# One forward substitution for all eight chunks of a pair of heads, instead of one for each half of four

## The chip, the cores and the metric

The kernel runs on one core of one Trainium2 chip. The metric is the device time of one launch in microseconds (us), the median of several runs. The engines are named as the profile names them: PE is TensorE's matmul, PEld its weight load, DVE is VectorE, ACT is ScalarE, POOL is GpSimd, SP issues the DMAs. A line such as L783 is a line of the profiled kernel.

## The reference, cut to what matters

One decoder layer at 512 tokens and width 2048, all in float32:

```python
h = modulate(rms_norm(x, norm_mix_g), sh_m, sc_m)
p = h @ w_in                                   # columns: RG-LRU, its gate, RWKV-7
y_a = rg_lru(conv(p_lru)) * gelu(p_gate)       # 1024 channels
y_b = rwkv7_mix(p_rwkv)                        # 1024 channels, 16 heads of 64
x = x + g_m * (concat(y_a, y_b) @ w_out)
h = modulate(rms_norm(x, norm_ffn_g), sh_f, sc_f)
x = x + g_f * ((silu(gate) * up) @ w_down)     # gate, up = h @ w_gu
return rms_norm(x, final_norm_g)
```

Inside `rwkv7_mix` a head's 64 x 64 state goes through the tokens one at a time:

```python
sa = state @ (-kk_t)
state = state * d_t + sa (kk_t * a_t)^T + v_t k_t^T
y_t = state @ r_t
```

## The kernel before, in words

Features lie on the 128 partitions, the 512 tokens on the free axis. A float32 product is made of three products of exactly split operands (`mm3`, L124 to L126), each 128x128 by 128x512. I call one of these three a large product. Weights come in by SP (L115), are rounded by ACT (L105), and DVE makes the remainder (L106).

The recurrence is done in chunks of 64 tokens, eight chunks, for two heads at a time (a pair; there are eight pairs). For each chunk and head it needs the inverse of a unit triangular 64 x 64 matrix I - A. This is done by a forward substitution in the two diagonal 32-blocks, on DVE, and by two small products for the block below them.

For each pair these pieces run:

- `rwkv_main`: what all tokens need (decays, normalized keys), once per pair.
- `rwkv_half`: operands and products of four chunks (L609 to L657), twice per pair. Its products are L624 (values by token), L633 and L643 (products within the chunks), L655 (transposes). `rw_dg` holds the diagonal 32-blocks.
- `inverse`: directly behind each `rwkv_half`. DVE spreads the blocks by a transpose (`rw_at`, L757), sets `rw_x` from a constant (L760), and makes 31 steps of a product (L764, `rw_xp`) and a sum (L766, `rw_x`). Two more transposes give `rw_xn` (L768) and `rw_xs` (L771). POOL copies `rw_xs` into `bd_xt` (L775). TensorE makes the lower block by L783 and L793, with ACT copies behind each (L787, L796).
- `rwkv_chain`: the state goes through the eight chunks one after the other. In each chunk, w = a product of the state (L694, L696) copied by ACT (L698), u = `bd_xt` times w (L701) copied by ACT (L703), the new state (L708, L709 on TensorE, L719 on ACT, L720 on DVE), and the output (L710, L712, L713). At the end a group norm and a gate (L729 to L745), and `y` is written to DRAM (L746).

The order is set by `weave`. It holds several generators in a list, traces the next step of the first one that may run by its own clock (constants such as `INVLAT`), and otherwise one step of a filler: three large products of work that does not hang on the chain. The filler has the rest of the input projection, the RG-LRU half, and the products of `y_a` with its half of `w_out` (`project(self.ya, 1, "mm")`). When all of `weave` has been traced, `channel` begins: it reads `y_b` back from DRAM (L439, tiles `yraw`, `yhi`, `ylo`), multiplies it with the other half of `w_out`, and makes the norm (L230, L240) and the feed-forward part. A scheduler may still move instructions within an engine. Each engine then works its own queue in order.

A pair's second half may be built only when the previous pair's chain has left the last chunk, because `bd_a`, `bd_bt` and `bd_v` are held once per half; the first half, when it has left the fourth.

Of the kernel before, what the change touches and what calls it, by code (L numbers as in the profile page):

```python
# [17 lines left out]
P = 128  # L18
S = 512
# [32 lines left out]
for _n, _k in _VEC:  # L52
# [4 lines left out]
# columns of the constants (shapes alone)  # L57
_CON = [("ident", 128), ("center", 128), ("bones", 128),
        ("gmask", 128), ("xinit", 128), ("m01", 2)]
# [8 lines left out]
def _constants():  # L68
    con = np.zeros((P, NCON), np.float32)
    p = np.arange(P)  # L70
    blk = (p[:, None] // C == p[None, :] // C).astype(np.float32)
    con[:, _COFF["ident"]:][:, :P] = np.eye(P, dtype=np.float32)
    con[:, _COFF["center"]:][:, :P] = np.eye(P, dtype=np.float32) - blk / C
    con[:, _COFF["bones"]:][:, :P] = blk
    s, t = (p % C)[:, None], np.arange(C)[None, :]
    con[:, _COFF["gmask"]:][:, :C] = s < t
    con[:, _COFF["gmask"] + C:][:, :C] = s <= t
    r = ((p % 32) // 4)[:, None, None]
    con[:, _COFF["xinit"]:][:, :P] = (
        np.arange(32)[None, :, None] == 8 * np.arange(4)[None, None, :] + r).reshape(P, P)  # L80
    q = (p // 32) % 2
    con[:, _COFF["m01"]] = q == 0
    con[:, _COFF["m01"] + 1] = q == 1
    return con


class Layer:
# [24 lines left out]
    def load_split(self, src, n):  # L112
        """src: DRAM [128, n] -> (hi, lo) float32r tiles [128, n]"""
# [14 lines left out]
    def gemm_steps(self, ps, src, acts):  # L128
        """ps[128, S] = W^T acts, src: DRAM [128, nk * 128], acts: list of (hi, lo); yields after each k"""
# [44 lines left out]
    def mod_pair(self, j):  # L174
        """columns j and j + 16"""
# [11 lines left out]
    def mod_steps(self, js, pool, tags):  # L187
        """the same for many columns, a quarter of c at a time"""
# [22 lines left out]
    def mod_scale(self, col, sc, g):  # L211
        """col = g * (1 + mod[:, sc])"""
# [3 lines left out]
    def square(self, acc, x, k, pool):  # L216
        """acc += x * x"""
# [7 lines left out]
    def norm(self, acc, tag):  # L225
        """1 / rms of each token, in all partitions (PSUM), from sums of squares by partition"""
# [16 lines left out]
    def modulate(self, x, col, rstd, sh, lo=None):  # L243
        """hi, lo of x * col * rstd + sh"""
# [54 lines left out]
    def mixing(self):  # L299
# [22 lines left out]
                # seven tiles stay in PSUM, four more take turns in the last bank by quarters of K  # L322
# [43 lines left out]
    def rwkv_weave(self, kvr0, kvr1, u0):  # L366
# [16 lines left out]
        def filler():  # L383
# [15 lines left out]
            # half of the channels through the output projection  # L399
# [23 lines left out]

        def chains():
            for pr in range(NPAIR):
                yield 0, 0, lambda: done["inv"] > 2 * pr
# [3 lines left out]
        self.weave([chains(), halves(0), halves(1), mains(), mods()], self.filler)  # L430
# [14 lines left out]
    def project(self, ys, half, *tags):  # L445
        """x1 += g_m * (ys through their half of w_out)"""
# [29 lines left out]
    def rwkv_setup(self, ctx):  # L476
# [4 lines left out]
        # zero at the first token of each chunk  # L481
# [3 lines left out]
        # block-diagonal operands (two heads); what lies off the blocks stays zero  # L485
# [36 lines left out]
    def rwkv_main(self, pr):  # L522
        """what a pair of heads needs of all the tokens"""
# [16 lines left out]
        # decay and its running product within a chunk  # L540
# [21 lines left out]
        # kk = k * k_k over its norm per head  # L562
# [15 lines left out]
        # k' = k (1 + (a - 1) k_a), the bonus, v by tokens  # L578
# [17 lines left out]
    def rwkv_half(self, pr, hf):  # L596
        """four chunks of a pair"""
# [21 lines left out]
        # v by tokens, centred over its features  # L619
# [9 lines left out]
        # products within the chunks  # L629
# [6 lines left out]
        d = rw.tile([P, 4, 32], F32, tag=f"dg{hf}", name="rw_dg")  # L636
# [40 lines left out]
        # through the chunks  # L677
# [49 lines left out]
        # group norm (y is centred already), bonus, gate  # L727
# [22 lines left out]
    def inverse(self, hf, dg, gb):  # L750
        """bd["xt"][hf]: the transposed inverse of I - A of each head and chunk, A^T in gb[:, :, :C]"""
# [3 lines left out]
        # diagonal 32-blocks, one to a partition (eight partitions share its columns)  # L755
        at = rw.tile([P, 32, 32], F32, tag=f"at{hf}", name="rw_at")
        nc.vector.transpose(  # L757
            out=at, in_=dg.rearrange("p c t -> p t c").unsqueeze(2).to_broadcast([P, 32, 8, 4]))
        x = rw.tile([P, 32, 4], F32, tag=f"x{hf}", name="rw_x")
        nc.vector.tensor_copy(out=x.rearrange("p t j -> p (t j)"), in_=self.con("xinit"))  # L760
# [6 lines left out]
        xn = rw.tile([P, 32, 4], F32, tag=f"at{hf}", name="rw_xn")      # [t, j, chunk]  # L767
        nc.vector.transpose(out=xn.rearrange("p (j r) c -> p j (r c)", r=8),  # L768
                            in_=x.rearrange("p t j -> p j t"))
        xs = rw.tile([P, 4, 32], F32, tag=f"dg{hf}", name="rw_xs")      # [j, chunk, t]  # L770
        nc.vector.transpose(out=xs, in_=xn.rearrange("p j c -> p c j"))  # L771
        xt = self.bd["xt"][hf]
        for g in range(4):
            rows = slice(g * 32, g * 32 + 32)
            nc.gpsimd.tensor_scalar(out=xt[rows, :, rows], in0=xs[rows], scalar1=1.0,  # L775
                                    scalar2=None, op0=ALU.mult)
        yield 0, INVLAT, None
        # lower left blocks: X21 = X22 A21 X11
        ps = self.ps("gr").rearrange("p (c x) -> p c x", x=P)
        for c in range(4):  # L780
            for g in range(2):
                q0, q1 = slice(g * C, g * C + 32), slice(g * C + 32, g * C + C)
                mm(ps[q1, c, :32], lhsT=gb[q0, c, 32:C], rhs=xn[q0, :, c], start=True, stop=True)  # L783
        rt = rw.tile([P, 4, 32], F32, tag=f"x{hf}", name="rw_rt")
# [3 lines left out]
        yield 0.43, HOP, None  # L788
        ps = self.ps("gr").rearrange("p (c x) -> p c x", x=P)
        for c in range(4):  # L790
# [3 lines left out]
        for g in range(2):  # L794
# [251 lines left out]
```

## Time and profile before

| | us |
|---|---|
| median of 3 runs | 2511.28 (2510.93 to 2513.99) |
| span of the profiled execution | 2515.8 |
| PE busy in the span | 2413.9 (96%) |
| DVE busy in the span | 1380.4 (55%) |
| ACT busy, POOL busy | 843.7 (34%), 82.0 (3%) |

The profiled execution is one run of its own; the page gives its span, from the first to the last instruction, and no other time for it. It stands 4.5 us above the median of the runs. Three stages matter here. Until about 225 us the input is normalized and the first products are made. From 225 to 939 us `weave`'s steps and filler run. From 939 us the products of `y_b` follow (norm at 1041 us), and then the feed-forward part to the end.

### The profile page before, as it was taken

Reading aid. Unit: us, or ns where it says so; the run is one execution under the profiler, and the core shown is the slowest. Engines: PE = TensorE matmul, PEld = TensorE weight load, DVE = VectorE, ACT = ScalarE, POOL = GpSimd, SP = SyncE. Lnnn points to the kernel's source line nnn. Section 1 sums busy time; section 2 is a strip of 40 time slices with the busy share of each in tenths; the row PEclk is TensorE's granted clock in tenths of the full one; section 3 lists DMA queues with packets and bytes.
Section 4 is the critical chain, followed back from the end, with each engine's and each line's share of the span. In section 5 each row is a group of like instructions: output and inputs, shape, how many; then the busy total and the mean of one; then the engine's idle time right before and its main releaser. Section 6 shows DMA issues by size and latency. Waiting matters only on the chain.

```text
span 2515.8 us, 30983 instructions
## 1 busy us (share of the span) xinstructions
PE 2413.9 (96%) x11560; PEld 1953.4 (78%) x11560; DVE 1380.4 (55%) x3111; ACT 843.7 (34%) x1340; POOL 82.0 (3%) x131
## 2 busy tenths in 40 slices
PE   5999999999999999899999999999999999999997
PEld 3677777877777886687788888888888888888885
DVE  7979898999969847854423322233322233222244
ACT  4357364455355333432222222222222222222221
POOL 0000111111101000000000000000000000000000
PEclk9999998999999999999999999999999999999998
DMA  8864444444342438366423332323333233333233
GB/s 304 308 219 130 148 128 143 131 152 144 125 135 81 143 108 283 119 195 194 160 90 95 108 100 93 101 83 98 106 98 99 89 92 105 101 93 100 85 95 112
DMA packets 138938, 333.22 MB, mean 132 GB/s; under 512 B 15458, under 2 KB 28898, under 8 KB 134690
## 3 DMA queue, kind: packets, MB, share of 16 engines
q1 hardware_dynamic: 138788, 331.25, 40.7%
q8 instruction: 90, 1.47, 0.2%
q14 instruction: 60, 0.49, 0.1%
HBM read 322.92 MB, written 7.87 MB: 131 GB/s over the span
## 4 chain that ended last, share of the span: by engine, by line
PE 72%; DVE 9%; DMA 7%; issue 1%; ACT 1%; SPq 0%; POOL 0%; DVEq 0%; ACTq 0%
PE ps_mm L124 10%; PE ps_mm L126 10%; PE ps_mm L125 10%; PE ps_gr L126 6%; PE ps_st L124 6%; PE ps_gr L124 6%; PE ps_st L126 6%; PE ps_gr L125 6%; PE ps_st L125 6%; DMA adaq<-in_w_ada 6%; DVE adaq L199 2%; DVE wlo L106 2%; DVE rw_xp L764 1%; DVE rw_x L766 1%; DMA wraw<-in_w_out 1%
## 5 line engine op out<-in xcount | busy, mean ns | idle before, releaser
L106 DVE TENSOR_TENSOR wlo<-wraw,whi 128x1024 fp32r<-128x1024 f32 (+2 forms) x552 | 496.7, 902 | 730.2 <-ACT whi L105 721.1
L105 ACT CAST whi<-wraw 128x1024 fp32r<-128x1024 f32 (+2 forms) x552 | 436.6, 792 | 1292.4 <-PE ps_mm L125 401.1
L124 PE MATMUL ps_mm<-hhi,whi 128*128 128x512 f32 x1020 | 417.1, 410 | 9.8 <-ACT hhi L251 7.2
L126 PE MATMUL ps_mm<-hhi,wlo 128*128 128x512 f32 x1020 | 407.2, 399 | 1.7 <-DVE wlo L106 1.6
L125 PE MATMUL ps_mm<-hlo,whi 128*128 128x512 f32 x1020 | 406.5, 399 | 0.8 <-DVE hlo L252 0.7
L124 PEld LDWEIGHTS ps_mm<-hhi,whi 128*128 128x128 f32 x1020 | 193.4, 190 | 53.2 <-ACT hhi L251 9.9
L125 PEld LDWEIGHTS ps_mm<-hlo,whi 128*128 128x128 f32 x1020 | 193.7, 190 | 43.4 <-DVE hlo L252 4.8
L126 PEld LDWEIGHTS ps_mm<-hhi,wlo 128*128 128x128 f32 x1020 | 193.8, 190 | 42.3 <-DVE wlo L106 3.0
L199 DVE SCALAR_TENSOR_TENSOR adaq<-adaq,cbq 128x512 f32<-128x512 f32 x256 | 173.5, 687 | 92.9 <-DMA adaq<-in_w_ada 85.1
L126 PE MATMUL ps_gr<-hhi,wlo 128*128 128x512 f32 x496 | 193.7, 390 | 3.1 <-DVE wlo L106 3.1
L126 PE MATMUL ps_st<-hhi,wlo 128*128 128x512 f32 x496 | 193.6, 390 | 2.0 <-DVE wlo L106 2.0
L124 PE MATMUL ps_st<-hhi,whi 128*128 128x512 f32 x496 | 194.0, 391 | 1.6 <-ACT hhi L251 1.6
L125 PE MATMUL ps_gr<-hlo,whi 128*128 128x512 f32 x496 | 193.5, 390 | 0.0
L125 PE MATMUL ps_st<-hlo,whi 128*128 128x512 f32 x496 | 193.5, 390 | 0.0
L124 PE MATMUL ps_gr<-hhi,whi 128*128 128x512 f32 x496 | 192.6, 391 | 0.0
L126 PEld LDWEIGHTS ps_gr<-hhi,wlo 128*128 128x128 f32 x496 | 93.4, 188 | 23.6 <-DVE wlo L106 4.1
L126 PEld LDWEIGHTS ps_st<-hhi,wlo 128*128 128x128 f32 x496 | 93.4, 188 | 21.8 <-DVE wlo L106 2.5
L124 PEld LDWEIGHTS ps_st<-hhi,whi 128*128 128x128 f32 x496 | 93.5, 188 | 21.6 <-ACT hhi L251 2.2
L125 PEld LDWEIGHTS ps_gr<-hlo,whi 128*128 128x128 f32 x496 | 93.7, 189 | 19.6
L124 PEld LDWEIGHTS ps_gr<-hhi,whi 128*128 128x128 f32 x496 | 93.7, 189 | 19.4
L125 PEld LDWEIGHTS ps_st<-hlo,whi 128*128 128x128 f32 x496 | 93.3, 188 | 19.8 <-DVE hlo L252 0.3
L766 DVE TENSOR_TENSOR rw_x<-rw_x,rw_xp 128x27 f32<-128x27 f32 (+23 forms) x496 | 94.7, 196 | 5.7
(312 smaller groups left out, 3809.6 us busy)
## 6 DMA issues: line engine op xcount, KB each, us to landing
wraw<-in_w_gu SPq DMA_DIRECT2D x176, 512.0 KB, 3.6
adaq<-in_w_ada SPq DMA_DIRECT2D x256, 256.0 KB, 3.3
wraw<-in_w_in SPq DMA_DIRECT2D x160, 256.0 KB, 3.0
ada<-in_w_ada SPq DMA_DIRECT2D x32, 1024.0 KB, 7.2
wraw<-in_w_down SPq DMA_DIRECT2D x64, 512.0 KB, 3.5
wraw<-in_w_out SPq DMA_DIRECT2D x64, 256.0 KB, 3.3
wraw<-in_w_down SPq DMA_DIRECT2D x64, 192.0 KB, 2.3
x<-in_x SPq DMA_DIRECT2D x32, 256.0 KB, 5.3
```

Source lines behind the costliest of these rows:

```text
L105: nc.scalar.copy(out=hi, in_=src)
L106: nc.vector.tensor_tensor(out=lo, in0=src, in1=hi.bitcast(F32), op=ALU.subtract)
L124: mm(ps, lhsT=w[0], rhs=x[0], start=start, stop=False)
L125: mm(ps, lhsT=w[0], rhs=x[1], start=False, stop=False)
L126: self.pe = mm(ps, lhsT=w[1], rhs=x[0], start=False, stop=stop).ins
L199: nc.vector.scalar_tensor_tensor(out=t, in0=t, scalar=1.0, in1=cb, op0=ALU.mult, op1=ALU.mult, accum_out=part[:, m, h:h + 1])
L764: tt(out=pr[:, :n, :j], in0=at[:, s + 1:, s:s + 1].to_broadcast([P, n, j]), in1=x[:, s:s + 1, :j].to_broadcast([P, n, j]), op=ALU.mult)
L766: tt(out=x[:, s + 1:, :j], in0=x[:, s + 1:, :j], in1=pr[:, :n, :j], op=ALU.add)
```

## The change

`inverse` is taken out of `rwkv_half` and becomes a generator of its own, one step of which runs when both halves of a pair are built. It substitutes for all eight chunks at once: each partition now holds one of 4 groups of columns instead of 8, and step s works on `s // 4 + 1` columns instead of `s // 8 + 1`. The chain of a pair starts when the whole inverse is done, where before it started when the first half's was done and asked for the second at chunk 4. `INVLAT` goes from 30.2 to 24.0.

```diff
-INVLAT = 30.2                   # substitution in the diagonal blocks
+INVLAT = 24.0
...
+        def inverses():
+            for pr in range(NPAIR):
+                yield 0, 0, lambda: done["built"] == 2 * pr + 2
+                yield from self.inverse(*self.pairs[pr][-1])
+
         def chains():
             for pr in range(NPAIR):
-                yield 0, 0, lambda: done["inv"] > 2 * pr
+                yield 0, 0, lambda: done["inv"] > pr
                 yield from self.rwkv_chain(pr)
...
-        self.weave([chains(), halves(0), halves(1), mains(), mods()], self.filler)
+        self.weave([chains(), inverses(), halves(0), halves(1), mains(), mods()], self.filler)
...
-        d = rw.tile([P, 4, 32], F32, tag=f"dg{hf}", name="rw_dg")
+        if hf == 0:
+            parts.append(rw.tile([P, NCH, 32], F32, tag="dg", name="rw_dg"))
+        d = parts[0][:, 4 * hf:4 * hf + 4]
...
-        yield from self.inverse(hf, d, gb)
...
-            if c == 4:
-                yield 0, 0, lambda: self.done["inv"] >= 2 * pr + 2
-            ar, gb, rkt, bn, kn = parts[hf]
+            ar, gb, rkt, bn, kn = parts[1 + hf]
...
-            out=at, in_=dg.rearrange("p c t -> p t c").unsqueeze(2).to_broadcast([P, 32, 8, 4]))
-        x = rw.tile([P, 32, 4], F32, tag=f"x{hf}", name="rw_x")
-        pr = rw.tile([P, 31, 4], F32, tag=f"dg{hf}", name="rw_xp")
+            out=at, in_=dg.rearrange("p c t -> p t c").unsqueeze(2).to_broadcast([P, 32, 4, NCH]))
+        x = rw.tile([P, 32, 8], F32, tag="x", name="rw_x")
+        pr = rw.tile([P, 31, 8], F32, tag="xp", name="rw_xp")
         for s in range(31):
-            n, j = 31 - s, s // 8 + 1
+            n, j = 31 - s, s // 4 + 1
             tt(out=pr[:, :n, :j], in0=at[:, s + 1:, s:s + 1].to_broadcast([P, n, j]),
                in1=x[:, s:s + 1, :j].to_broadcast([P, n, j]), op=ALU.mult)
             tt(out=x[:, s + 1:, :j], in0=x[:, s + 1:, :j], in1=pr[:, :n, :j], op=ALU.add)
...
-        yield 0.43, HOP, None
+        yield 0.86, HOP, None
```

The two small products (L783 and L793 before, L788 and L798 after) now cover eight chunks in one step, and POOL's copies come eight in a row instead of four. TensorE has the same instructions as before, in another order; no DMA is added or taken away.

What stands in the queues shows where work moved. The line numbers of the changed kernel are some 5 higher. The first place is TensorE's queue at the end of the weave. Before, the last pair's gate (L743, L744), like every step of its chain ahead of it, stands between large products of the filler:

```order
L126 MATMUL ps_mm<-yhi,wlo 128x512
L743 MATMUL ps_ch<-lora_g,rw_lwg 128x512
L744 MATMUL ps_ch<-lora_s,rw_lws 128x512
L124 MATMUL ps_mm<-yhi,whi 128x512
L125 MATMUL ps_mm<-ylo,whi 128x512
```

In the changed kernel the filler's last large product (the first row) stands ahead of the last pair's second half (L629 to L662), its inverse (L788, L798) and its whole chain (from L705 on):

```order
L126 MATMUL ps_mm<-yhi,wlo 128x512
L629 MATMUL ps_st<-cons,mix_v 64x64 x8
L638 MATMUL ps_gr<-rw_ar,bd_b_1390 128x128 x4
L650 MATMUL ps_gr<-rw_ar,bd_k_1392 128x128 x4
L747 MATMUL ps_ch<-lora_g,rw_lwg 128x512
L748 MATMUL ps_ch<-lora_s,rw_lws 128x512
L662 MATMUL ps_st<-cons,bd_b_1390 128x128 x4
L698 MATMUL ps_ch<-bd_v_1402,bd_bt_1398 128x128
L662 MATMUL ps_st<-cons,bd_k_1392 128x128 x4
L714 MATMUL ps_y<-rw_rkt,bd_v_1402 128x64
L788 MATMUL ps_gr<-rw_xn,rw_gb 32x32 x16
L798 MATMUL ps_gr<-rw_xs,rw_rt 32x32 x16
```

From L705 on, eight chunks and the group norm follow without one large product among them; the next one is the first of `y_b`. Before, 39 large products of the filler were left behind the last pair's gate (L744).

The second place is DVE's queue in the substitution. Before, for instance in the sixth pair, steps of the substitution (here the last ones of a half) stand among weight splits (L106) and partial columns of the modulation (L199):

```order
L766 TENSOR_TENSOR rw_x<-rw_x,rw_xp 128x16
L199 SCALAR_TENSOR_TENSOR adaq,adaparts<-adaq,cbq 128x512
L764 TENSOR_TENSOR rw_xp<-rw_at,rw_x 128x12
L766 TENSOR_TENSOR rw_x<-rw_x,rw_xp 128x12
L764 TENSOR_TENSOR rw_xp<-rw_at,rw_x 128x8
```

In the changed kernel's last pair the steps stand alone from the third of the 62 on, up to the two transposes:

```order
L768 TENSOR_TENSOR rw_xp<-rw_at,rw_x 128x16
L770 TENSOR_TENSOR rw_x<-rw_x,rw_xp 128x16
L768 TENSOR_TENSOR rw_xp<-rw_at,rw_x 128x8
L770 TENSOR_TENSOR rw_x<-rw_x,rw_xp 128x8
L772 STREAM_TRANSPOSE rw_xn<-rw_x 128x256
```

In the other seven pairs the substitution still stands among splits and modulation columns, and 123 to 208 large products stand on TensorE between a pair's second half (L650) and its L788.

More of the change, by code (lines that the diff above doesn't have):

```diff
@@ L58 @@
 _CON = [("ident", 128), ("center", 128), ("bones", 128),
-        ("gmask", 128), ("xinit", 128), ("m01", 2)]
+        ("gmask", 128), ("xinit", 256), ("m01", 2)]
 _COFF = {}
@@ L77, in _constants @@
     con[:, _COFF["gmask"] + C:][:, :C] = s <= t
-    r = ((p % 32) // 4)[:, None, None]
-    con[:, _COFF["xinit"]:][:, :P] = (
-        np.arange(32)[None, :, None] == 8 * np.arange(4)[None, None, :] + r).reshape(P, P)
+    r = ((p % 32) // 8)[:, None, None]
+    con[:, _COFF["xinit"]:][:, :256] = (
+        np.arange(32)[None, :, None] == 4 * np.arange(8)[None, None, :] + r).reshape(P, 256)
     q = (p // 32) % 2
@@ L748, in rwkv_chain, with inverse @@
         yield 1.07, 2.0, None
-    def inverse(self, hf, dg, gb):
+    def inverse(self, dg, *parts):
         nc, rw = self.nc, self.rw
@@ L754, in inverse @@
         tt = nc.vector.tensor_tensor
-        at = rw.tile([P, 32, 32], F32, tag=f"at{hf}", name="rw_at")
+        at = rw.tile([P, 32, 32], F32, tag="at", name="rw_at")
         nc.vector.transpose(
-            out=at, in_=dg.rearrange("p c t -> p t c").unsqueeze(2).to_broadcast([P, 32, 8, 4]))
-        x = rw.tile([P, 32, 4], F32, tag=f"x{hf}", name="rw_x")
-        nc.vector.tensor_copy(out=x.rearrange("p t j -> p (t j)"), in_=self.con("xinit"))
-        pr = rw.tile([P, 31, 4], F32, tag=f"dg{hf}", name="rw_xp")
+            out=at, in_=dg.rearrange("p c t -> p t c").unsqueeze(2).to_broadcast([P, 32, 4, NCH]))
+        x = rw.tile([P, 32, 8], F32, tag="x", name="rw_x")
+        nc.vector.tensor_copy(out=x.rearrange("p t j -> p (t j)"), in_=self.con("xinit", 256))
+        pr = rw.tile([P, 31, 8], F32, tag="xp", name="rw_xp")
         for s in range(31):
-            n, j = 31 - s, s // 8 + 1
+            n, j = 31 - s, s // 4 + 1
             tt(out=pr[:, :n, :j], in0=at[:, s + 1:, s:s + 1].to_broadcast([P, n, j]),
@@ L766, in inverse @@
             tt(out=x[:, s + 1:, :j], in0=x[:, s + 1:, :j], in1=pr[:, :n, :j], op=ALU.add)
-        xn = rw.tile([P, 32, 4], F32, tag=f"at{hf}", name="rw_xn")
-        nc.vector.transpose(out=xn.rearrange("p (j r) c -> p j (r c)", r=8),
+        xn = rw.tile([P, 32, NCH], F32, tag="at", name="rw_xn")
+        nc.vector.transpose(out=xn.rearrange("p (j r) c -> p j (r c)", r=4),
                             in_=x.rearrange("p t j -> p j t"))
-        xs = rw.tile([P, 4, 32], F32, tag=f"dg{hf}", name="rw_xs")
+        xs = rw.tile([P, NCH, 32], F32, tag="xp", name="rw_xs")
         nc.vector.transpose(out=xs, in_=xn.rearrange("p j c -> p c j"))
[L772 to L776, printed above, removed]
+        for hf in range(2):
+            for g in range(4):
+                rows = slice(g * 32, g * 32 + 32)
+                nc.gpsimd.tensor_scalar(out=self.bd["xt"][hf][rows, :, rows], in0=xs[rows, 4 * hf:4 * hf + 4],
+                                        scalar1=1.0, scalar2=None, op0=ALU.mult)
         yield 0, INVLAT, None
-        ps = self.ps("gr").rearrange("p (c x) -> p c x", x=P)
-        for c in range(4):
+        ps = self.ps("gr").rearrange("p (c x) -> p c x", x=C)
+        for c in range(NCH):
+            gb = parts[c // 4][1]
             for g in range(2):
                 q0, q1 = slice(g * C, g * C + 32), slice(g * C + 32, g * C + C)
-                mm(ps[q1, c, :32], lhsT=gb[q0, c, 32:C], rhs=xn[q0, :, c], start=True, stop=True)
-        rt = rw.tile([P, 4, 32], F32, tag=f"x{hf}", name="rw_rt")
+                mm(ps[q1, c, :32], lhsT=gb[q0, c % 4, 32:C], rhs=xn[q0, :, c], start=True, stop=True)
+        rt = rw.tile([P, NCH, 32], F32, tag="x", name="rw_rt")
         for g in range(2):
@@ L787, in inverse @@
             nc.scalar.copy(out=rt[q1], in_=ps[q1, :, :32])
-        yield 0.43, HOP, None
-        ps = self.ps("gr").rearrange("p (c x) -> p c x", x=P)
-        for c in range(4):
+        yield 0.86, HOP, None
+        ps = self.ps("gr").rearrange("p (c x) -> p c x", x=C)
+        for c in range(NCH):
             for g in range(2):
@@ L793, in inverse @@
                 mm(ps[q0, c, :32], lhsT=rt[q1, c, :], rhs=xs[q1, c, :], start=True, stop=True)
-        for g in range(2):
-            q0, q1 = slice(g * C, g * C + 32), slice(g * C + 32, g * C + C)
-            nc.scalar.copy(out=xt[q0, :, q1], in_=ps[q0, :, :32])
-        yield 0.43, 1.4, None
+        for hf in range(2):
+            for g in range(2):
+                q0, q1 = slice(g * C, g * C + 32), slice(g * C + 32, g * C + C)
+                nc.scalar.copy(out=self.bd["xt"][hf][q0, :, q1], in_=ps[q0, 4 * hf:4 * hf + 4, :32])
+        yield 0.86, 1.4, None
         self.done["inv"] += 1
```

## The prediction

> **What bounds the kernel now.** I read the page first, then the busy time by stage, then TensorE's waits in the stage that the change touches. The page says that TensorE is the bound of the whole:
>
> ```profile
> span 2515.8 us, 30983 instructions
> PE 2413.9 (96%) x11560; PEld 1953.4 (78%) x11560; DVE 1380.4 (55%) x3111; ACT 843.7 (34%) x1340; POOL 82.0 (3%) x131
> ```
>
> By stage (span, then busy time of each engine, granted clock, DMA share, GB/s) it is less simple:
>
> ```profile
> 225.00:939.00 714.00, 685.63 (x4048) 550.23 (x4043) 602.99 (x1967) 350.68 (x689) 71.32 (x106) 0.97 0.41 128
> 939.00:1041.00 102.00, 92.76 (x387) 70.76 (x387) 78.39 (x182) 35.32 (x56) 0.00 (x0) 1.00 0.76 253
> 1041.00:2516.00 1475.00, 1446.69 (x6368) 1194.86 (x6368) 514.80 (x656) 350.90 (x426) 0.00 (x0) 0.99 0.34 107
> ```
>
> The first row is the weave. TensorE is busy for 686 of 714 us, DVE for 603, and the granted clock is 0.97. DVE's load is the one that the change lowers. So the next view is what TensorE waits for there (total us, times, longest), and what one such wait does, by the timeline and by two stretches around it:
>
> ```profile
> PE ps_gr L783 <- DVE rw_xn L768: 18.7, 8, 3.7
> PE ps_st L568 <- ACT rw_t L566: 2.5, 2, 2.2
> PE ps_gr L783 <- DVE rw_x L766: 0.6, 1, 0.6
> ...
> 433.23 0.66 PE L783 MATMUL ps_gr<-rw_xn,rw_gb 32*32 32x32 f32 x16 [3.71 <-DVE rw_xn L768]
> ...
> 433.00:443.00 10.00, 9.77 (x51) 6.31 (x52) 5.95 (x23) 6.54 (x13) 2.84 (x4) 0.51 0.46 140
> 443.00:453.00 10.00, 10.00 (x64) 8.72 (x63) 9.24 (x36) 5.81 (x13) 0.00 (x0) 1.00 0.39 128
> ```
>
> TensorE waits 19.3 us (18.7 + 0.6) for the substitution's result, in nine of its sixteen halves. Behind the 3.71 us wait the clock is 0.51 for 10 us, so it costs about 5 us more. Over the stage, 0.03 of 714 us is 21 us lost to the clock, and I put it all down to these waits. The price of DVE's lateness is then about 19 + 21 = 40 us. The rest of the 714 us is TensorE's own work, so relief of DVE can take about 40 us and no more.
>
> **The change, part by part.**
>
> *DVE's work.* Where a half's step stands alone, starts follow each other by the dependence and not by the size:
>
> ```profile
> 843.05 0.20 DVE L766 TENSOR_TENSOR rw_x<-rw_x,rw_xp 128x45 f32<-128x45 f32 x1
> 843.29 0.20 DVE L764 TENSOR_TENSOR rw_xp<-rw_at,rw_x 128x42 f32<-128x42 f32 x1
> 843.53 0.20 DVE L766 TENSOR_TENSOR rw_x<-rw_x,rw_xp 128x42 f32<-128x42 f32 x1
> ...
> 850.65 0.17 DVE L764 TENSOR_TENSOR rw_xp<-rw_at,rw_x 128x12 f32<-128x12 f32 x1
> 850.86 0.17 DVE L766 TENSOR_TENSOR rw_x<-rw_x,rw_xp 128x12 f32<-128x12 f32 x1
> ```
>
> That is 0.24 us at 42 elements and 0.21 at 12. The new shapes have 8 to 76 elements, mean 50 (1560 elements in 31 steps, against 920 before). The slope of 0.03 us in 30 elements gives 0.24 to 0.25 at 50. So 62 steps take about 15 us per pair where two halves took twice 14. On DVE the change saves some 13 us per pair of steps alone in the queue, and about 2 us for the second spreading transpose, 8 x 15 = 120 us at most. It saves less where another instruction stands between two steps, since then the wait was filled.
>
> *The waits at L783.* Eight inverses remain where sixteen were, and the last pair's is counted below. With 7/16 of the 40 us they would cost 18. DVE has less behind it, so I take 11 left: a gain of 29 us. The bounds are 40 (none left) and 10 (each of the seven waits is as long as the 3.71 us one, clock included).
>
> *The tail.* In the new order the filler's last large product stands ahead of the last pair's second half. From there until `y_b`'s products nothing covers the chain. I add up that stretch from rows of before, starting at the second half's first product (L624):
>
> ```profile
> 852.06 0.69 PE L624 MATMUL ps_st<-cons,mix_v 128*64 128x64 f32 x16
> 852.67 1.16 PE L633 MATMUL ps_gr<-rw_ar,bd_b 128*128 128x128 f32 x8
> 853.67 1.06 PE L643 MATMUL ps_gr<-rw_ar,bd_k 128*128 128x128 f32 x8
> 856.34 0.60 PE L655 MATMUL ps_st<-cons,bd_b 128*128 128x128 f32 x4
> 857.93 2.05 DVE L757 STREAM_TRANSPOSE rw_at<-rw_dg 128x1024 f32<-128x1024 f32 x1
> 862.82 0.65 PE L783 MATMUL ps_gr<-rw_xn,rw_gb 32*32 32x32 f32 x16
> 864.98 0.44 PE L793 MATMUL ps_gr<-rw_xs,rw_rt 32*32 32x32 f32 x16
> 865.47 0.52 ACT L796 COPY bd_xt<-ps_gr 32x128 f32<-32x128 f32 x2 [0.68 <-PE ps_gr L793]
> ...
> L775 POOL TENSOR_SCALAR bd_xt<-rw_xs 32x128 f32<-32x128 f32 x64 | 39.9, 623 | 287.2 <-DVE rw_xs L771 142.1 <-DVE rw_xp L764 123.9 <-DVE rw_x L766 17.8
> ...
> 570.52 0.38 PE L701 MATMUL ps_ch<-rw_w,bd_xt 128*128 128x128 f32 x2
> 570.74 0.39 PE L708 MATMUL ps_ch<-bd_v,rw_kn 128*128 128x128 f32 x2
> 571.26 0.49 PE L709 MATMUL ps_ch<-rw_u,rw_bn 128*128 128x128 f32 x2
> 572.13 0.35 DVE L720 SCALAR_TENSOR_TENSOR rw_s<-ps_ch,rw_pcs,rw_w 128x128 f32<-128x128 f32 x1
> 572.73 0.38 PE L696 MATMUL ps_ch<-rw_s,bd_a 128*128 128x128 f32 x2
> 572.95 0.33 PE L710 MATMUL ps_y<-rw_rkt,bd_v 128*128 128x64 f32 x2
> 573.12 0.39 PE L712 MATMUL ps_y<-rw_ar,rw_s 128*128 128x64 f32 x2
> 573.64 0.39 PE L701 MATMUL ps_ch<-rw_w,bd_xt 128*128 128x128 f32 x2
> ...
> 923.66 1.02 PE L732 MATMUL ps_ch<-rw_t,cons 128*128 128x512 f32 x2
> 929.32 1.02 PE L743 MATMUL ps_ch<-lora_g,rw_lwg 128*128 128x512 f32 x2
> 931.50 0.33 SPq L746 DMA_DIRECT2D y<-rw_t  x1
> 937.06 1.20 ACT L105 CAST yhi<-yraw 128x512 fp32r<-128x512 f32 x2
> ...
> 939.28 0.39 PE L124 MATMUL ps_mm<-yhi,whi 128*128 128x512 f32 x1
> 1040.88 1.07 PE ps_ch L230 x8
> ```
>
> 1. L624 to the spreading transpose: 857.93 - 852.06 = 5.9 us, with the same group norm of the pair before between them on DVE.
> 2. The transpose 2.0, what is left of that norm 2.2 (four instructions of 0.3 to 0.7), 62 steps 14.9, the transpose to `rw_xn` 0.5: 19.6, so `rw_xn` stands at 25.5 us.
> 3. L783 to L793 2.2, to ACT's copies 0.5, two copies 0.5: 28.7. POOL's first four copies (4 x 0.62, behind `rw_xs` at about 26) end at the same time; the other four are needed only at chunk 4.
> 4. Seven chunks at 3.12 us (573.64 - 570.52, a pair with little between its steps) and a last one of 1.3, with the norm's square: 21.8 + 1.3 + 0.7, so L732 stands at 52.5 us.
> 5. L732 to the write of `y`: 7.8 before, less some 1.9 us of splits and `x1` sums that are no longer between, plus about 1 for a halved clock: 7.0, so the write is issued at 59.5 us.
> 6. From that write to the norm: 1040.88 - 931.50 = 109.4 us as before. SP goes straight from the write to the reads of `y_b` (yhi 5.6 us later), DVE and ACT go from the gate to the splits, and the loads and modulation columns that paced that stage before follow in the same order. I add 2 us for large products that begin at a low clock.
>
> The sum is 171 us from the filler's last product to the norm. Before, from the filler's last product (939.28) to the norm was 101.6 us. The tail adds 69 us. For the chunk I take the 3.12 us: closest in kind, since hardly anything stands between its steps. Its bounds are 2.5 (0.4 us between the end of L709 and L720 and 0.2 us between the end of L720 and L696, in which other work went ahead) and 3.5 (clock at a half, 0.2 us more on two products of the cycle). Seven chunks make that -4 to +3 us, and steps 3 and 5 are open by 3 us each.
>
> *The covered work that goes.* The last pair's second half, inverse and chain were between filler products and took TensorE's time there. From start to start these are 0.6 + 1.0 + 1.0 + 2 x 0.5 for the half and 2 x (0.6 + 0.4) for the inverses. A chunk has five wide fp32 products (0.22, L701 to L708) and three narrow ones (0.17, L710 to L712), 1.6, eight times 12.9; norm and gate take 2 x 1.0. Together that is 21 us that the covered stretch no longer holds. They are inside the 171.
>
> *Costed at nothing.* POOL's eight copies in a row: 5 us, of which chunk 0 needs the first four, and filler products lie behind L788 in the first seven pairs. The first chunks of a pair wait for the whole inverse: the filler covers it until it runs out, and that is the tail. SP: no DMA is added, and what is queued behind a waiting one is a weight load that runs three tiles ahead.
>
> On the clock the row is 0.51 for 10 us behind a 3.71 us wait. The Trainium skill (TensorE: Matmul & The Clock Gate, Part 1) says that the array falls to half speed after an idle window of about 3.4 us and comes back after as long a busy one. By it the whole substitution in the tail (some 17 us without a product) ends at half clock, and the chunks may stay there: 3.5 us each, a sum 3 us above mine; were the clock full, 4 us below. The trace agrees on the fall; no row here shows a chain of small products alone.
>
> **The sum.** +69 (tail) - 21 (moved out of the covered stretch) - 29 (waits and clock) = +19 us. Against the profiled execution that is a span of 2535; the runs' median is 4.5 lower, so 2511.3 + 19 = 2530.
>
> **The rivals.**
>
> *DVE was the true bound, and the tail is cheap* (faster). The place is the tail, its price 69. For it: DVE is busy 84% of the weave, and all nine waits are for it. If all 40 us go and the tail is 10 us shorter: 69 - 10 - 21 - 40 = -2. It decides in favour of faster only if the tail adds less than 61 at full gain, or less than 50 at mine. Against it: each step of the tail is a row, and a chain of 8 chunks is on it. At its end, 20 us off the tail, the time is 2499.
>
> *Gain and tail cancel* (no change): 2506 to 2516, which needs 14 us off my sum, for instance all waits gone and a tail of 65.
>
> *The waits stay* (slower still). For it: one late inverse now holds up eight chunks, and L788's place in the queue is set by estimates, as L783's was. Seven waits with their clock, 7 x 5 = 35 us, leave a gain of 5, and the sum is +43: 2554.
>
> *The change does not reach the queue*: the order shows that it does. I give it nothing.
>
> **How the numbers follow.** The forecast, slower by 8 to 32 us (2519 to 2543), has 0.62; the waits staying, over 2543, 0.16; cancelling, 0.12; faster by over 5 us (0.2%, about what a measurement of this kernel tells from no change) 0.08. The rest, slower by 5 to 8, has 0.02. Faster is then 0.08, same 0.12, slower 0.80. The range leaves out one in ten on each side: 2508 to 2553. The predicted time is the forecast's 2530.
>
> **What the changed profile would show.** If I am right, the slices of TensorE's busy time have one hollow stretch of about 60 us, from about 890 to 950 us, with some 17 us nearly empty first and small products alone after that, at a lowered clock; TensorE's longest waits are L788 on `rw_xn` once for some 17 us, and L705, L713 and L700 on ACT and DVE in the last pair. The filler's last large product ends at about 890 instead of 939 us (939 - 21 - 29), the norm L230 stands at about 1060. DVE's busy time falls by 70 to 120 us, and the other seven waits for `rw_xn` sum to under 8 us. I would be wrong if large products stood in the tail, if the filler's end came before 870 (DVE held up more than its waits show), or if the seven waits were as long as before.

## The result and the profile after

The changed kernel takes 2557.82 us (median of 4 runs, 2553.32 to 2559.96), the kernel before 2511.86 beside it: a ratio of 1.018, 95% interval 1.0165 to 1.0194. That is 46 us slower, where 19 were forecast. The direction and the place were right; the size was not, and the time lies 5 us above the forecast's range.

The page's head and three of its rows in 40 slices (64 us each; 9 is 90% or more):

```profile
span 2558.2 us, 30462 instructions
PE 2422.3 (95%) x11560; PEld 1966.9 (77%) x11560; DVE 1315.8 (51%) x2583; ACT 843.3 (33%) x1324; POOL 76.4 (3%) x131
...
PE   5999999999999967899999999999999999999997
...
PEclk9999999999999968999999999999999999999998
DMA  8864455545224206636623333323333323332233
```

DVE has 65 us less to do and the span is 42 longer. The slices show the hollow: in the slice from 895 to 959 us TensorE has a 6 and the clock a 6, and hardly a byte moves (DMA 0); TensorE's 7 and 8 follow behind it. By stage (span, busy time of PE, PEld, DVE, ACT and POOL, clock, DMA share, GB/s), with the borders at the filler's last large product, the last norm of the recurrence and the norm L230:

```profile
225.00:904.50 679.50, 652.61 (x3829) 525.88 (x3828) 510.22 (x1347) 337.58 (x638) 61.59 (x98) 0.98 0.42 133
904.50:964.00 59.50, 36.76 (x229) 32.05 (x229) 26.17 (x87) 11.16 (x36) 4.18 (x8) 0.60 0.03 11
964.00:1085.00 121.00, 97.65 (x392) 75.60 (x391) 82.09 (x187) 37.56 (x59) 0.00 (x0) 0.92 0.68 217
1085.00:2558.00 1473.00, 1447.15 (x6368) 1195.56 (x6367) 515.00 (x656) 351.15 (x426) 0.00 (x0) 0.99 0.34 107
```

The second row is the new one. Its 59.5 us hold 229 products, nearly all small, at a clock of 0.60. Inside it (start, length, what; waits in brackets):

```profile
904.46 0.69 PE L629 MATMUL ps_st<-cons,mix_v 128*64 128x64 f32 x16
929.93 1.15 PE L788 MATMUL ps_gr<-rw_xn,rw_gb 32*32 32x32 f32 x32 [19.37 <-DVE rw_xn L772]
933.70 0.77 PE L705 MATMUL ps_ch<-rw_w,bd_xt 128*128 128x128 f32 x2 [0.70 <-ACT bd_xt L802]
937.73 0.80 PE L705 MATMUL ps_ch<-rw_w,bd_xt 128*128 128x128 f32 x2
...
961.85 0.49 PE L705 MATMUL ps_ch<-rw_w,bd_xt 128*128 128x128 f32 x2
963.81 1.12 PE L736 MATMUL ps_ch<-rw_t,cons 128*128 128x512 f32 x2 [0.69 <-ACT rw_t L733]
...
914.44 56.32 SPq L750 DMA_DIRECT2D y<-rw_t  x2
...
1084.76 1.05 PE L230 MATMUL ps_ch<-ones,sqacc 128*128 128x1 f32 x8 [2.29 <-DVE sqacc L223]
```

(The SP row joins the writes of the last two pairs; the second one is issued at 914.44 + 56.32 - 0.33 = 970.4.) TensorE waits 19.37 us for the substitution, then eight chunks follow at (961.85 - 933.70) / 7 = 4.02 us each. Against the kernel before:

| | before | after | difference | forecast |
|---|---|---|---|---|
| filler's last large product | 939.28 | 904.46 | -34.8 | -50 (= -21 - 29) |
| from there to the norm L230 | 101.6 | 180.3 | +78.7 | +69 |
| norm L230 | 1040.88 | 1084.76 | +43.9 | +19 |

The 21 us of the last pair's work did leave the covered stretch, so that stretch gained 34.8 - 21 = 14 us by itself, not 29. What TensorE waited for in it (total, times, longest; the window ends at the filler's last product):

```profile
PE ps_gr L788 <- DVE rw_xn L772: 9.0, 7, 2.6
PE ps_st L573 <- ACT rw_t L571: 7.9, 6, 2.6
PE ps_st L592 <- DVE rw_t L589: 3.8, 5, 2.0
PE ps_ch L700 <- DVE rw_s L724: 2.3, 3, 1.7
```

The waits for the substitution fell from 19.3 to 9.0 us. But two products of `rwkv_main`, L573 and L592 (L568 and L587 before), now wait 11.7 us where it was 2.5. All rows of this view sum to 26.8 us, against 28.1 before. The clock loses 11.9 us there, against 23.9.

### The profile page after: what moved, and what is told of

It is laid out like the page before. It is cut to its first block, busy times and chain, and to the rows that moved or that the text cites. A ratio compares the mean times of both kernels' runs of the same rounds, so it can differ in the third digit from the quotient of the medians.

```text
span 2558.2 us, 30462 instructions
## 1 busy us (share of the span) xinstructions
PE 2422.3 (95%) x11560; PEld 1966.9 (77%) x11560; DVE 1315.8 (51%) x2583; ACT 843.3 (33%) x1324; POOL 76.4 (3%) x131
## 4 chain that ended last, share of the span: by engine, by line
PE 68%; DVE 13%; DMA 9%; issue 2%; ACT 2%; POOL 0%; SPq 0%; DVEq 0%; ACTq 0%
PE ps_mm L124 8%; PE ps_mm L125 8%; PE ps_mm L126 8%; DMA adaq<-in_w_ada 7%; PE ps_gr L125 6%; PE ps_gr L124 6%; PE ps_gr L126 6%; PE ps_st L125 6%; PE ps_st L124 6%; PE ps_st L126 6%; DVE adaq L199 2%; DVE wlo L106 2%; DVE rw_x L770 1%; DVE rw_xp L768 1%; DMA cbq<-csilu 1%
## 5 line engine op out<-in xcount | busy, mean ns | idle before, releaser
L106 DVE TENSOR_TENSOR wlo<-wraw,whi 128x512 fp32r<-128x512 f32 (+2 forms) x552 | 497.2, 903 | 737.2 <-ACT whi L105 727.6
L105 ACT CAST whi<-wraw 128x512 fp32r<-128x512 f32 (+2 forms) x552 | 437.1, 793 | 1327.9 <-PE ps_mm L125 434.2
L124 PE MATMUL ps_mm<-hhi,whi 128*128 128x512 f32 x1020 | 411.9, 405 | 8.4 <-ACT hhi L251 6.9
L124 PEld LDWEIGHTS ps_mm<-hhi,whi 128*128 128x128 f32 x1020 | 192.8, 189 | 53.4 <-ACT hhi L251 9.4
L199 DVE SCALAR_TENSOR_TENSOR adaq<-adaq,cbq 128x512 f32<-128x512 f32 x256 | 173.5, 690 | 108.9 <-DMA adaq<-in_w_ada 93.9
L124 PE MATMUL ps_st<-hhi,whi 128*128 128x512 f32 x496 | 194.0, 391 | 1.6 <-ACT hhi L251 1.6
L124 PE MATMUL ps_gr<-hhi,whi 128*128 128x512 f32 x496 | 192.7, 391 | 0.0
L124 PEld LDWEIGHTS ps_st<-hhi,whi 128*128 128x128 f32 x496 | 93.6, 189 | 21.5 <-ACT hhi L251 2.2
L124 PEld LDWEIGHTS ps_gr<-hhi,whi 128*128 128x128 f32 x496 | 93.7, 189 | 19.3
L124 PE MATMUL ps_gr<-shi,whi 128*128 128x512 f32 x242 | 94.1, 389 | 0.0
```

Source lines behind the costliest of these rows:

```text
L105: nc.scalar.copy(out=hi, in_=src)
L106: nc.vector.tensor_tensor(out=lo, in0=src, in1=hi.bitcast(F32), op=ALU.subtract)
L124: mm(ps, lhsT=w[0], rhs=x[0], start=start, stop=False)
L199: nc.vector.scalar_tensor_tensor(out=t, in0=t, scalar=1.0, in1=cb, op0=ALU.mult, op1=ALU.mult, accum_out=part[:, m, h:h + 1])
```

## The experiments

The theory at this point (T): the loss is the uncovered tail. The chain starts later in the order, so the filler is used up before the last pair. Its rivals: the joint substitution costs time in itself (D), or the gain under cover was eaten by new waits (M). All times are medians, with the ratio to the kernel before and its 95% interval. In kernels with inserted lines the numbers are up to 11 higher; the names in the rows say which is meant.

**1. The tail covered, in both kernels.** 336 large products are added at the filler's end.

```diff
             yield from self.project(self.ya, 1, "mm")
+            for n in range(112):
+                p = self.ps("mm")
+                self.mm3(p, (self.ya[n % 8][0][:, :P], self.ya[n % 8][1][:, :P]), self.ya[(n + 3) % 8], True, True)
+                yield
```

> The kernel before with 336 added large products at the filler's end (112 steps of three, on operands that are there, nobody uses the sums). At 0.217 us a product that is 72.8 us of work on TensorE. In the kernel before the filler already outlasts the last chain, so the work can hide nothing: every theory expects +73 us (2584), within 3 us. The run is the yardstick for its sister on the changed kernel.

> The changed kernel with the same 336 products. They stand between the last pair's chunks in the queue, up to the last chunk. Theory T (the loss is the uncovered tail, and the covered stretch gained some 12 us): the tail's 38 idle us and its half clock vanish under them, the filler ends at about 904.5 + 72.8 + 21 = 998 us, and the time is 12 to 14 us UNDER the filled kernel before: about 2571, only +13 on the changed kernel. Theory F (the forecast's own numbers, 29 us gained under cover): 29 under the filled kernel before, 2555. Theory M (the waits moved to rwkv_main and ate the whole gain): level with the filled kernel before, 2584. Theory D (the longer steps on DVE cost time in themselves): over 2590.

Measured: before with the products 2573.48 us (1.0247, 1.0223 to 1.0271), after with them 2590.32 (1.0321, 1.0294 to 1.0349). The last added product, the write of the last `y` and the norm, first in the kernel before, then in the changed one:

```profile
1013.68 0.39 PE L126 MATMUL ps_mm<-yhi,ylo 128*128 128x512 f32 x1
...
929.61 0.33 SPq L752 DMA_DIRECT2D y<-rw_t  x1
...
1104.95 1.55 PE L230 MATMUL ps_ch<-ones,sqacc 128*128 128x1 f32 x8 [2.29 <-DVE sqacc L223]
```

```profile
1000.00 0.39 PE L126 MATMUL ps_mm<-yhi,ylo 128*128 128x512 f32 x1
...
999.76 0.33 SPq L756 DMA_DIRECT2D y<-rw_t  x1
...
1114.03 1.85 PE L230 MATMUL ps_ch<-ones,sqacc 128*128 128x1 f32 x8 [2.29 <-DVE sqacc L223]
```

The 72.8 us of products cost the kernel before only 62, since the stage behind them shrank from 101.6 to 91 us. With the same work in both, the changed kernel's filler ends 13.7 us earlier. That is the gain under cover, measured by itself, so M's "whole gain" falls. Yet the time is 17 us longer, which T had not expected. It is the time that D had named (over 2590), but D's ground, longer steps that cost time in themselves, does not fit a filler that ends earlier. The stage behind starts differently: 91 us from the last added product to the norm in the first kernel, where the last `y` was written long before; 114.3 us from the write in the second, where the write comes last. In the unfilled changed kernel the same stretch is 1084.76 - 970.4 = 114.3. So a late last chain costs twice: the tail, and a slower start of the next stage.

The waits of these two, before and after the change (225 to 1000 us):

```profile
PE ps_gr L789 <- DVE rw_xn L774: 18.7, 10, 5.1
PE ps_st L574 <- ACT rw_t L572: 2.6, 2, 2.2
```

```profile
PE ps_gr L794 <- DVE rw_xn L778: 8.9, 7, 2.4
PE ps_st L579 <- ACT rw_t L577: 7.1, 6, 1.9
PE ps_st L598 <- DVE rw_t L595: 3.4, 4, 1.8
```

In sum 28.1 against 25.0 us of waits, and 17.1 against 11.9 us lost to the clock: 8 of the 13.7 us. Where the other 5 or 6 come from these views do not show.

**2. The later start alone.** The kernel before, where a chain may start only with both halves' inverses; nothing else is touched.

```diff
-                yield 0, 0, lambda: done["inv"] > 2 * pr
+                yield 0, 0, lambda: done["inv"] >= 2 * pr + 2
```

> The kernel before, substitution in halves as it was, but each pair's chain is put into the order only when BOTH halves' inverses are there. It changes only the place of the chain in the order. Theory T: the chain of each pair comes later against the filler, the filler runs out before the last chain as in the changed kernel, and with no gain under cover the time is 2511 + 35 to 65 = 2546 to 2576, with L783/L788-like waits unchanged. Theory D (the joint substitution itself costs, not the later start): within 8 us of 2511.

Measured: 2558.92 us (1.0189, 1.0164 to 1.0214). The same loss as the change, with the substitution in halves as it was. The filler's last product is at 910, the norm where the tail puts it:

```profile
927.86 38.80 SPq L746 DMA_DIRECT2D y<-rw_t  x2
...
1080.34 1.86 PE L230 MATMUL ps_ch<-ones,sqacc 128*128 128x1 f32 x8 [2.29 <-DVE sqacc L223]
```

From the last write (966.3) to the norm is 114.0 us again. So the later start of the chains is by itself enough to make the loss. In the profiled executions the joint substitution ends the filler some 6 us earlier (904.5 for 910.6) and then takes some 10 us longer to the norm (180 for 170): what it saves is about what its slower tail (next) costs. The exchange of waits comes with the later start too: here L783 waits 12.7 us for `rw_xn`, and L568 and L587 wait 9.4, where the kernel before has 19.3 and 2.5.

**3. The clock in the tail.** The changed kernel with products that nobody uses in the last pair alone: 72 ahead of L788, and one behind each step of the chain (`self.warm(1)`).

```diff
+    def warm(self, n):
+        if self.done["built"] == 2 * NPAIR and self.done["out"] == NPAIR - 1:
+            for _ in range(n):
+                self.nc.tensor.matmul(self.ps("mm"), lhsT=self.ya[0][0][:, :P], rhs=self.ya[3][0],
+                                      start=True, stop=True)
```

> The changed kernel, with products that nobody uses in the last pair's uncovered stretch alone: 72 large ones (15.6 us at full clock) before L788, and one after each step of the chain, each in a gap where TensorE waits for ACT or DVE. They are to hold the clock up. Theory C (the chunk took 4.02 us instead of 3.12 because of the half clock): granted clock near 1.0 from L788 to L736, chunks of 3.1 to 3.4 us, the time 5 to 8 us lower: about 2551. Theory L (the chunk is set by the latencies between the engines, whatever the clock): chunks of 3.8 to 4.1 us, time within 2 us of 2558 or over it, as the added products now stand in the way.

Measured: 2549.94 us (1.0154, 1.0132 to 1.0175), 7.9 under the changed kernel. First two chunks with such products between them, then two without (the scheduler had moved theirs ahead):

```profile
933.27 0.38 PE L706 MATMUL ps_ch<-rw_w,bd_xt 128*128 128x128 f32 x2
936.15 0.38 PE L706 MATMUL ps_ch<-rw_w,bd_xt 128*128 128x128 f32 x2
...
949.88 0.49 PE L706 MATMUL ps_ch<-rw_w,bd_xt 128*128 128x128 f32 x2 [0.18 <-ACT rw_w L702]
952.56 0.49 PE L706 MATMUL ps_ch<-rw_w,bd_xt 128*128 128x128 f32 x2 [0.18 <-ACT rw_w L702]
```

At full clock a chunk takes 2.88 us with the added products and 2.68 without, against 4.02 in the changed kernel. Theory C holds, with chunks still shorter than its 3.1 to 3.4 us.

**4. The later start for the last pair only.**

```diff
-                yield 0, 0, lambda: done["inv"] > 2 * pr
+                yield 0, 0, lambda: done["inv"] >= 2 * pr + (2 if pr == NPAIR - 1 else 1)
```

> The kernel before, with the later start (both halves' inverses must be there) for the LAST pair's chain alone; the first seven pairs start as they did. Theory A (the tail is the sum of eight delays: in the order's own times a pair takes 87 to 90 us after the change and 73 before, so the filler is used up by seven earlier pairs): only one delay is left, the write of the last y comes 8 to 15 us later than 931.5, and the time is 2511 + 8 to 15 = 2519 to 2526. Theory B (the last pair's own wait for its whole inverse makes the tail): as bad as holding all eight, 2550 or more.

Measured: 2528.78 us (1.0071, 1.0047 to 1.0095), 17 us over the kernel before. The write of the last `y` is at 945.11, 13.6 us later, and the norm at 1059.07, another 114.0 behind it. That is a little over the 8 to 15 of theory A and far from B: something over a third of the loss is the last pair's own delay, and the rest is what the pairs ahead of it had piled up.

**5. Faster chains.** `weave`'s constants for a chunk are made smaller, so that less filler goes between its steps; in a second kernel the steps of `rwkv_main` also come later.

```diff
-HOP = 1.10
+HOP = 0.65
-LM1, LM2, LM3 = 4.2, 6.8, 9.0
+LM1, LM2, LM3 = 6.8, 9.4, 9.0          # e7 alone
-LSN = 1.79
+LSN = 1.30
```

> The changed kernel with two of the planner's numbers smaller: HOP 0.65 for 1.10, LSN 1.30 for 1.79, so each chunk of a chain is followed by three fewer steps' worth of filler and the last chain ends, in the order's own times, at 644 us and not 745 (before: 642). Theory T: the tail is covered again, y_87 is written near 925 us, the tail's +79 us are gone but for the 21 us of the last pair's own products, and what is left is the gain under cover: 9 to 14 us under the kernel before, 2498 to 2503, if the chunks' steps don't begin to wait. Theory W (a step that comes 0.65 us after the one before waits for ACT's copy each time): 64 chunks with two such waits of 0.2 to 0.3 us, 25 to 40 us, so 2525 to 2540.

> The kernel before with the same two numbers (HOP 0.65, LSN 1.30). It has no uncovered tail to lose: its last chain ends 21 us earlier in the order's own times. Theory T: the write of y_87 comes earlier than the filler's end by 20 us or more, the stage behind it is then limited by the filler's end, and the time is 0 to 6 us under 2511. Theory W: 25 to 40 us over 2511.

> The changed kernel with HOP 0.65, LSN 1.30 and, beside them, LM1 6.8 for 4.2 and LM2 9.4 for 6.8: the second and third step of rwkv_main come four filler steps later, so L573 and L592 should find their operands. Theory M (the gain under cover was eaten by the new waits of these two products, 8.1 and 3.8 us, and the clock behind them): both waits under 2 us in sum and the time 8 to 14 us under that of the same kernel with LM1 4.2. Theory N (DVE's queue only moves its lateness to the next reader): the waits reappear elsewhere and the time is within 4 us of it.

Measured: 2535.93 us (1.0101, 1.0084 to 1.0118) after the change, 2524.53 (1.0048, 1.0031 to 1.0065) before it, 2552.89 (1.017, 1.0155 to 1.0185) with the later `rwkv_main`. The first took 22 us off the changed kernel: the tail is covered and the last write stands at 947.94. But under cover it lost what T had not counted:

```profile
PE ps_mm L124 <- ACT lru_g L878: 13.8, 4, 6.1
PE ps_gr L788 <- DVE rw_xn L772: 11.1, 6, 3.5
PE ps_mm L124 <- DVE mix_r L477: 5.6, 2, 3.2
```

Waits of 44.5 us and 27.3 for the clock, where the changed kernel has 26.8 and 11.9. These are not the chain's own copies, as theory W had it (L705 on `rw_w` 3.3 us), but large products that wait for ACT's gates and DVE's mixing. With later steps of `rwkv_main`, L573 and L592 still wait (5.9 and 7.2 us): M's remedy made it worse. In the kernel before, whose tail was covered already, the quicker constants cost 13 us, between what T and W had said.

**6. `rwkv_main` kept away from the substitution.** In the order of DVE, the next pair's `rwkv_main` stands among the 62 steps. Here it may start only behind the pair's inverse: with the tail covered, after the change and before it, and with the faster chains.

```diff
-                yield 0, 0, lambda: done["built"] >= 2 * pr and len(self.kvr) > pr and done["out"] >= pr - 1
+                # in the kernel before: done["inv"] >= 2 * pr
+                yield 0, 0, lambda: done["inv"] >= pr and len(self.kvr) > pr and done["out"] >= pr - 1
```

> The changed kernel with the 336 added products (so that no tail is open), and rwkv_main of the next pair may be put into the order only when the pair's inverse is done; in the changed kernel it begins with the inverse, and its steps on DVE stand among the 62 steps of the substitution. Theory Q (the gain under cover came to 9 us and not 29 because these two share DVE's queue: the substitution's result is late by main's steps, and main's products by the substitution): waits at L788 from 8.9 to under 4 us, at L573 and L592 from 10.5 to under 3, clock loss from 11.9 to under 6; the filler ends some 15 us earlier than 1000.4, and the time is 10 to 20 us under the 2590 of the same kernel without the hold. Theory N (DVE's lateness only moves to the next reader): waits of 20 us or more in sum, time within 5 us of 2590.

> The kernel before with the 336 products and the same hold on rwkv_main (both inverses of the pair done). Its two substitutions keep the whole 124 steps. Theory Q: the waits at L783 fall too, from 18.7 to about 10, but less is gained than after the change, since two blocks of steps remain: 5 to 15 us under the 2573 of the same kernel without the hold. Theory N: within 5 us of 2573.

> The changed kernel without added products, with HOP 0.65 and LSN 1.30 (which closed the tail but began new waits: 2536) and the hold on rwkv_main. Theory Q: the waits of that kernel at L788, L573 and L592 (18 us) fall to under 6, with the clock behind them 10 to 20 us under 2536, that is 2516 to 2526. Theory N: within 5 us of 2536. Only if the waits at the gates' PSUM tiles (13.8 us) go too is it under the kernel before.

Measured: 2615.08 us (1.0416, 1.0381 to 1.045), 25 over the filled changed kernel; 2586.17 (1.0308, 1.028 to 1.0335), 13 over the filled kernel before; 2528.81 (1.008, 1.0057 to 1.0104), 7 under the one with faster chains. Theory Q falls. The last run is no exception: the waits that Q meant (L788, L573, L592) went from 18.1 to 20.7 us there, and those for ACT's gates from 13.8 to 2.4. In the first, L579 and L598 (L573 and L592) wait less, and L794 (L788) more than before:

```profile
PE ps_gr L794 <- DVE rw_xn L778: 13.5, 4, 5.6
PE ps_gr L794 <- DVE rw_pcs L569: 5.7, 1, 5.7
PE ps_st L579 <- ACT rw_t L577: 4.0, 1, 4.0
```

With the same work on every engine, waits and clock loss went from 25.0 + 11.9 to 38.8 + 32.4 us.

**7. DVE's load cut in steps.** The filled kernels, with fewer of the 31 steps of each substitution.

```diff
-        for s in range(31):
+        for s in range(15):          # 23 in e13
```

> The changed kernel with the 336 added products, and only the first 15 of the 31 steps of each substitution (the blocks' inverses stay incomplete: that part of the computation is left out). DVE has some 8 us less to do for each pair, 60 us in all, and nothing else changes. Theory P (the price that the forecast read from the waits was right, about 37 us of waits and clock in this kernel too, and the joint substitution takes only part of DVE's lateness away): with half the steps gone waits and clock fall from 37 to under 15, and the time is 18 to 28 us under 2590. Theory G (waits are set by where steps meet in DVE's queue and not by how much stands there): a fall of less than 10 us, or none.

> The kernel before with the 336 products and only the first 15 of the 31 steps in each half's substitution (the rest of the inverses is left out). DVE has some 14 us less for each pair, 100 us in all. Theory P: of the 45 us of waits and clock over 35 go, so 30 to 40 us under 2573. Theory G: a fall of less than 15 us.

> As the first of these runs, with 23 of the 31 steps (the last eight left out; they are also the shortest in rows). Theory P: between the two, 8 to 15 us under 2590. Theory G: within 8 us of 2590, on either side.

Measured: after the change 2583.01 us with 15 steps (1.0279, 1.0262 to 1.0296) and 2583.37 with 23 (1.0282, 1.0262 to 1.0302), both 7 under the full count; before the change 2554.22 with 15 (1.017, 1.0147 to 1.0193), 19 under. With 15 steps after the change no wait for `rw_xn` is left, and others have taken its place:

```profile
PE ps_ch L706 <- DVE rw_s L730: 9.5, 6, 2.7
PE ps_st L598 <- DVE rw_t L595: 7.2, 6, 1.6
PE ps_st L579 <- ACT rw_t L577: 6.6, 6, 1.9
PE ps_mm L124 <- DVE mix_r L483: 4.3, 3, 2.9
```

Waits sum to 29.1 us, more than with all the steps (25.0); the clock loses 8.5 for 11.9, and the filler ends 2.8 us earlier. In the kernel before, half of all steps gone was worth 15.7 us at the filler's end. Its wait for `rw_xn` is all but gone there, and the state's is the longest:

```profile
PE ps_gr L789 <- DVE rw_xn L774: 0.7, 1, 0.7
PE ps_ch L702 <- DVE rw_s L726: 5.6, 4, 3.2
```

That wait went from 18.7 to 0.7 us, but the sum of all waits only from 28.1 to 24.0, and the clock loss from 17.1 to 10.2. Theory G holds after the change; before it the result lies between the two.

**8. An earlier last write.** The kernel before, with the quicker constants (0.65, 0.65, 1.30) in the chain of the last pair, or of the last two.

```diff
-            yield 0.43, HOP, None
+            yield 0.43, 0.65 if pr >= NPAIR - 1 else HOP, None
...
-            yield 1.07, LSN, None
+            yield 1.07, 1.30 if pr >= NPAIR - 1 else LSN, None
```

> The kernel before, with HOP 0.65 and LSN 1.30 for the last pair's chain alone. Its eight chunks have some 13 us less of filler between them, and no other pair is touched. Theory E (the stage behind the weave starts from the write of y_87 and takes 109 to 114 us from there; it is not paced by the filler's end, from which the run with added products took 91): the write comes 8 to 13 us earlier than 931.5, the filler's end stays at 939.4, the norm stands at 1030 to 1036 and the time is 5 to 11 us under the kernel before, 2500 to 2506. Theory S (the loads and modulation columns pace that stage whatever the write does): within 3 us of 2511.

> The same for the last two pairs. The write comes another 10 us or so earlier; by theory E the filler's end plus 91 us now sets the norm (1030), so little more is gained: 2498 to 2506, unless the quicker steps of the second chain begin to wait. Theory S: within 3 us of 2511.

Measured: 2510.44 us with the last pair (0.9986, 0.9975 to 0.9998), 2508.17 with two (0.9987, 0.9973 to 1.0), beside 2512.96 for the kernel before. The write and the norm of the first:

```profile
919.45 0.33 SPq L746 DMA_DIRECT2D y<-rw_t  x1
...
1033.95 1.87 PE L230 MATMUL ps_ch<-ones,sqacc 128*128 128x1 f32 x8 [2.29 <-DVE sqacc L223]
```

The write is 12.1 us earlier and the norm 6.9, though the profiled execution of the kernel before stood 4.5 us above its median. A second 12 us (write at 907.91) moved the norm no further (1034.8). So the norm came where theory E had put it, at 1030 to 1036, but of its 5 to 11 us in time only 2.5 came. The write sets the stage only while it is late; behind a filler that ends at 936 and 939, 98 and 96 us of that stage remain. These two are the only versions here that lie under both kernels, by a ratio of 0.1%, less than what this measurement can surely tell.

## Why the prediction was right and wrong

**Right.** The queue did what was read from it: `rw_xn` stood 25.5 us behind L629 as forecast, the first L705 at 29.2 for 28.7, and the write 6.6 us behind the last norm for 7.0. The late last chain is the cause: the later start alone makes the same loss (2), and with the tail covered 17 us of it remain, since the last write is still late (1).

**Wrong: the 29 us of waits and clock.** The step said: "I put it all down to these waits. The price of DVE's lateness is then about 19 + 21 = 40 us." The gain under cover was 13.7 us (1). The waits for the substitution did fall, to 9.0 us, where under 8 was forecast; that was not the error. The error was to take a wait that ends earlier as time gained. What stood behind it was nearly as late and waited next: L573 and L592 after the change, and the chain's product with the state (L700, in (7) L706 and L702) when the substitution's waits were gone. Taking half the steps out of the kernel before took 18 us of waits for `rw_xn` away and gave 4 us in the sum of waits and 19 in time, so 40 was at least not to be had by this means. This term is 15 of the 25 us by which the norm came later than forecast. Two of its readings do not come out of the rows either. Of the 23.9 us that the clock lost under cover before, 3.4 stand behind two other waits (L568 on `rw_t`, 2.17 us, and L124 on `mix_r`, 2.27 us). And the lower bound of 10 us, seven waits of 3.71 us with their clock, would be 7 x (3.71 + 5) = 61 us of waits, more than the 40 that they were to be taken from.

**Wrong: the chunk, 3.12 us.** It took 4.02, over the stated bound of 3.5; seven make 6.3 us. The bound added the half clock to two products of the cycle only. At half clock every one of the eight products counts, since in a bare chain nothing hides them: 1.34 us more, where the forecast had 1.6 us for all of them at full clock. At full clock the chunk is 2.68 us (3): the row that the 3.12 was taken from (573.64 - 570.52, with other work between) was too long for a bare chain at full clock and too short for one at half.

**Wrong by little: write to norm.** 114.3 for 109.4 + 2. It is 114.0 to 114.3 in (1), (2), (4) and the changed kernel, and 110 to 117 in the other runs whose last write came late.

15.2 + 6.3 + 2.9 make 24.4 of the 25 us at the norm. Between the medians the miss is 27, since the profiled execution before was 4.5 us above its median and the one after at its own.

**The rivals.** "The waits stay" gave 2554, nearest to the time, but by luck and not by its mechanism: the seven waits for `rw_xn` sum to 9.0 us with a clock loss of 11.9 in all, and not 35. "The tail is cheap" fell with (1) and (2). DVE's busy time fell by 65 us, under the 70 to 120 forecast.

**The clock rule.** The changed kernel's clock is 0.50 from 913.7 to 961.5 us. The Trainium skill (TensorE: Matmul & The Clock Gate, Part 1) puts the return to full speed after a busy window of about 3.4 us. The trace agrees on the fall in the tail, which comes 3.1 us after TensorE's last product (910.13 + 0.43 to 913.7). It does not agree on the return: between 930 and 958 us TensorE's records are busy for 26.4 of 28 us and the clock stays at half.

```profile
930.00:958.00 28.00, 26.40 (x161) 23.58 (x161) 2.65 (x7) 6.44 (x23) 4.18 (x8) 0.50 0.00 1
```

Open is which waits move where, and why: nothing tried made the waits of `rwkv_main` go without others growing. That the first seven pairs' delay is added up by the wait of a second half for the previous chain was read from the order and fits (4); giving the halves a third set of buffers was not tried, nor was `INVLAT` alone.

## What to carry to other kernels

A step that is merged to save work on a side engine can move the start of a serial chain to the later of its inputs; count how much filler is left when the last chain starts, because the delay adds up over all the turns and is paid once, at the end, without cover. A wait in a profile, with the clock lost behind it, is an upper bound for what its removal brings: look at what in the same queue would be late next, and take the bound itself only where nothing is. Where the last result of a stage starts the loads of the next, its time of writing is the number to watch, not the end of the filler.

## What was not expected of the hardware

A chain of small products that starts at half clock can stay there: 0.50 for 47.8 us, the last 31.6 of them with products (L788 at 929.93, full at 961.5). In (2) the like chain was at full clock 6.5 us after its first product (933.90 to 940.4), and in (3), never having fallen, it stayed at 1.00 while TensorE was busy for 9.25 of 11.5 us. What decides between them no run here shows. It may not be the kernel: of the changed kernel's four runs one has a mean granted clock of 0.980 (2553.32 us) and three 0.974 to 0.976, and of the four in (2) one has 0.980 (2552.33 us, the profiled one) and three 0.973 to 0.976. Only one execution of each was profiled.

The fall needs no long pause either. Under cover the changed kernel is at half clock six times (11.9 us lost), five of them beside a wait of 2.0 to 2.6 us and the sixth beside one of 0.9. In (2) the clock fell 0.8 us after a product (925.45 + 0.43 to 926.7), in 7 us of which TensorE was busy for 2.9:

```profile
920.00:927.00 7.00, 2.90 (x14) 1.59 (x12) 6.91 (x19) 2.10 (x4) 0.00 (x0) 0.98 0.03 9
927.00:934.00 7.00, 0.10 (x4) 0.10 (x6) 6.94 (x52) 0.27 (x1) 0.00 (x0) 0.50 0.10 37
```
